# One decoder layer on one core: the per-layer input gets a buffer of its own, and the first norm's rows move from ScalarE's queue to SyncE's

## The chip, the cores and the metric

The kernel runs on 1 core of one Trainium2 chip. Times are device microseconds (us) of one execution, from the device's own clock; the figure that counts is the median of several runs. PE is TensorE (matmuls; PEld its weight loads), ACT is ScalarE, DVE is VectorE, POOL is GpSimd, SP is SyncE, which here only issues transfers (DMAs). SPq, ACTq and POOLq are the queues on which these three engines issue them.

## The reference

One layer of a decoder trunk over 256 positions of width 1024, all in 32-bit floats. Three attention mixers share one projection; their outputs are gated and merged; two norms follow, with a feed-forward block between them that also takes a second, per-layer input `p` (256 positions of width 256):

```python
proj = x @ w_in[i]
...
o_a = dsa_mixer(aq, ak, av, iq, ik, iw, bias_a)
o_b = dilated_mixer(bq, bk, bv, bias_b)
o_c = moba_mixer(cq, ck, cv, bias_c)
gates = jax.nn.sigmoid(x @ w_gate[i]).reshape(bsz, s_len, N_BRANCH, D_MODEL)
merged = (gates[:, :, 0] * (o_a @ w_br_a[i])
          + gates[:, :, 1] * (o_b @ w_br_b[i])
          + gates[:, :, 2] * (o_c @ w_br_c[i]))
x = layer_norm(ALPHA * x + merged @ w_out[i], ln1_g[i], ln1_b[i])
h = jnp.square(jax.nn.relu(x @ w_up[i])) @ w_down[i]
ple = jax.nn.sigmoid(x @ w_ple_gate[i]) * (p[i] @ w_ple[i])
x = layer_norm(ALPHA * x + h + ple, ln2_g[i], ln2_b[i])
```

`w_ple_gate` is called the embedding gate here, and `p @ w_ple` the embedding product.

## The kernel before, in words

**Split operands.** Each 32-bit operand of a matmul is held as two parts: a high part, the value rounded to the narrower matmul format, and a low part, the rest. A product is three matmuls: high by high, high by low, low by high (`prod`, L136). The parts of a weight block are made on the chip. `Weights._split` loads a block of up to 128 x 1024 (512 KB) into `raw` (SP, L71), ACT copies it to the high part `whi` (L75), and DVE, up to the 58th block with POOL for some of the columns, subtracts it to get the low part `wlo` (L79). `raw` and the parts have five buffers each. `Weights.get` keeps some blocks ahead of the matmuls (`AHEAD`, four); a load waits until a `raw` buffer is free, so until its subtraction is done.

**Order.** The order of the work on each engine is made by a scheduler from the program order and priorities; each engine then works through its list strictly in order, and so does each queue of transfers. `issue_after(x)` makes what stands in its block come after the instruction `x` on the engine of `x`.

**The mixers.** Blocks of queries and keys (`feat`) are products of the weights with the input, `q_pair` (ACT L217, DVE L218) and `k_pair` (L228, L229) turn them into pairs, and `logits` (L274) multiplies them. Bias tables T come by DMA from a table in memory (`toeplitz`, three transfers each, L188; three buffers). `attend` transposes the weights of the softmax (L314), copies them into a pair `pt` (ACT L321, DVE L322), multiplies by the values (L324, L325) and adds the parts (ACT L328 and DVE L329 `ov`, DVE L330 `o`); `pair_out` (L333, L334) makes a pair of the result. Between these steps the program puts products of the gates (`fill("g")`, L241), which fill PE's time. After the scores of the indexer comes the second mixer (two rounds of `slots`), then the third mixer (three rounds of `head`), then the first.

**The per-layer input.** Between the second mixer and the third, `p` is loaded into `pr` (SP, L471), and the pair `ph` (ACT, L472) and `pl` (DVE, L473) is made of it. `pr` is a tile of the pool `wk2` under the tag `eb`, so it takes one of the two buffers of that tag, which hold the softmax weights of `slots`; its load waits until the transposes of the second round have read them. `ph` and `pl` are first read more than 100 us later, by the embedding product.

**The end of the first half.** `merge` multiplies the last branch (L582, L583), and makes pairs `q` of the merged values (L586, L587). `outp` is the output projection: eight blocks of `w_out` into four PSUM banks (halves b of the positions, halves c of the columns). `outp.finish` gets the last four blocks, and with them up to four further blocks from the list ahead: both of `w_ple` and the first two of the eight of the embedding gate (`u_pg`). As each bank is complete, `ln1` adds the residual (DVE L646, from PL, which ACT's queue loaded at L614), takes statistics (L623 to L629), a power on POOL (L630), and scales by the norm's two rows (DVE L635, L637); then PE transposes (L656) and a pair `x1` is made (ACT L658, DVE L659). The embedding product (24 matmuls, copied to PL by ACT at L675) fills PE meanwhile; the embedding gate `pg` reads `x1`. After it come 32 blocks of the feed-forward's first product (L705, L707), its second product, and the second norm.

**The rows.** `row_load` (L610) loads the two rows of a norm to all 128 partitions, 1024 KB, on ACT's queue. For the first norm it stands behind the load of the residual, and both are issued after the sixth of the eight high parts of the merge (`muls[5]`).

Of the kernel before, what the change touches and what calls it, by code (L numbers as in the profile page):

```python
# [11 lines left out]
F32 = mybir.dt.float32  # L12
F32R = mybir.dt.float32r
ALU = mybir.AluOpType
# [6 lines left out]
S = 256  # L21
# [10 lines left out]
N_U = 384  # L32
# [17 lines left out]
class Weights:  # L50


    def __init__(self, tc, raw, part):
        self.tc, self.nc = tc, tc.nc
        self.raw, self.part = raw, part
        self.units, self.done, self.parts, self.after = [], 0, {}, ()

    def add(self, src, n, hi=None, lo=None, stage=None, by="v", urgent=0):
        i = len(self.units)
# [3 lines left out]
    def _split(self, i):  # L63
        nc = self.nc
        src, n, hi, lo, r, by, _ = self.units[i]
        if callable(src):
            r = src()
        else:
            if r is None:
                r = self.raw.tile([128, 1024], F32, name="raw", tag="raw")[:, :n]  # L70
            nc.sync.dma_start(r, src)  # L71
        if hi is None:
            hi = self.part.tile([128, 1024], F32R, name="whi", tag="whi")[:, :n]
            lo = self.part.tile([128, 1024], F32R, name="wlo", tag="wlo")[:, :n]
        nc.scalar.copy(hi, r)  # L75
        cut = ((nc.vector, slice(None)),) if by == "v" else (
            (nc.vector, slice(0, by * n // 1024)), (nc.gpsimd, slice(by * n // 1024, n)))
        for e, c in cut:
            low = e.tensor_tensor(lo[:, c], r[:, c], hi[:, c].bitcast(F32), op=ALU.subtract)  # L79
            if e is nc.gpsimd:  # L80
                self.pool = low.ins
        self.parts[i] = (hi, lo)
# [13 lines left out]
def hybrid_layer(ctx: ExitStack, tc: tile.TileContext, x0, xn, pT, wqk, wva, wvb, wg, wbc, wba,  # L96
                 wout, wup, wdq, wdn, wpg, wple, lnrow, rel, mask, out):
    nc = tc.nc
    pe, act, dve, pool = nc.tensor, nc.scalar, nc.vector, nc.gpsimd
# [8 lines left out]
    W = Weights(tc, raw, part)  # L108
# [13 lines left out]
    ph = keep.tile([128, 2, S], F32R, name="ph")  # L122
    pl = keep.tile([128, 2, S], F32R, name="pl")
# [5 lines left out]
    t = banks.tile([128, 512], F32, name="b4", tag="b4")  # L129
# [23 lines left out]
    pm = mid.enter_context(tc.tile_pool(name="pm", bufs=1))  # L153
# [19 lines left out]
    for t in TASKS:  # L173
# [8 lines left out]
        else:  # L182
            u_q.append([add(wqk[int(t) - FIRST], 1024)])

    def toeplitz(h0, step):
        t = tp.tile([128, 3, 256], F32, name="T", tag="T")
        for i in range(3):
            nc.sync.dma_start(t[:, i], bass.AP(  # L188
                tensor=tabd.tensor,
                offset=tabd.offset + (h0 + i * step) * COPIES * N_U + 127,  # L190
                ap=[[N_U - 16, 8], [N_U - 1, 16], [1, 256]]))
        return t


# [87 lines left out]
    op = pm.tile([128, 8, 2, S], F32R, name="op")  # L282
# [20 lines left out]
            dve.tensor_tensor(V[:, b, h0:h0 + heads, DH:128], src,  # L303
                              V[:, b, h0:h0 + heads, 0:DH].bitcast(F32), op=ALU.subtract)

    n_pt = [0]

    def attend(heads, o):

        ts = []  # L310
        for i, (P, vh, h) in enumerate(heads):
            t = next(ps_t)
            for c in (1, 2, 0):
                m = pe.transpose(t[:, 128 * c:128 * c + 128], P[:, 128 * c:128 * c + 128], ident)  # L314
                if i or c != 1:
                    tc.keep_in_program_order(m)
            ts.append(t)
        for t, (P, vh, h) in zip(ts, heads):
            pt = pts[n_pt[0] % 2]
            n_pt[0] += 1  # L320
            act.copy(pt[:, 0], t[:, 0:384])  # L321
            dve.tensor_tensor(pt[:, 1], t[:, 0:384], pt[:, 0].bitcast(F32), op=ALU.subtract)  # L322
            v = next(ps_t).rearrange("p (a s) -> p a s", a=2)
            pe.matmul(v, lhsT=V[:, 0, vh], rhs=pt[:, :, 0:256], start=True, stop=False)  # L324
            pe.matmul(v[:, :, 128:256], lhsT=V[:, 1, vh], rhs=pt[:, :, 256:384], start=False,  # L325
                      stop=True)
            x = wk2.tile([64, 2, S], F32, name="ov", tag="ov")
            act.copy(x, v[64:128])  # L328
            dve.tensor_tensor(x, v[0:64], x, op=ALU.add)  # L329
            dve.tensor_tensor(o[64 * h:64 * h + 64], x[:, 0], x[:, 1], op=ALU.add)  # L330
# [99 lines left out]
    for j in range(4):  # L430
        s = logits(iq[j], kI)
        r = wk2.tile([128, 768], F32, name="ri", tag="eb")
# [23 lines left out]
    for j in range(2):  # L456
# [10 lines left out]
        slots(qs, k, Ts, 1 + 2 * j, o)  # L467
        pair_out(o, 3 + j)
        fill("g")
    pr = wk2.tile([128, 2, S], F32, name="pr", tag="eb")  # L470
    nc.sync.dma_start(pr, pT)  # L471
    act.copy(ph, pr)  # L472
    dve.tensor_tensor(pl, pr, ph.bitcast(F32), op=ALU.subtract)  # L473
    values(u_vb, 384, 5, 6, False)
    fill("g")
    for j in range(3):
# [61 lines left out]
    class Wide:  # L538
# [17 lines left out]
                for c in range(len(self.cut[b])):  # L556
                    self.go(k, b, c)

        def finish(self, ks, done, spare):

            for k in ks:
                self.ws[k] = W.get(self.units[k], min(AHEAD, ks[-1] - k + spare))
            for b in range(2):
                for c in range(len(self.cut[b])):
                    for k in ks:
                        self.go(k, b, c)
                    done(b, c, self.acc[b][c])
# [38 lines left out]
    x1 = p3.tile([128, 2, KT, 2, 128], F32R, name="x1")  # L606
    rows1 = p3.tile([128, 2, D], F32, name="rows", tag="rows")

    def row_load(t, i):
        act.dma_start(t, lnrow[i:i + 2].rearrange("r d -> (r d)").partition_broadcast(128)  # L610
                      .rearrange("p (r d) -> p r d", r=2))

    with tc.issue_after(muls[5]):
        act.dma_start(PL, xn)  # L614
        row_load(rows1, 0)

    st = {}

# [41 lines left out]
        if b == 1:  # L660
            W.after = (i0.ins, i1.ins)

    outp.finish((4, 5, 6, 7), ln1, 5)


    wp = [W.get(u, 0) for u in u_ple]
# [309 lines left out]
```

## Time and profile before

| what | us |
|---|---|
| median of 3 runs (438.4 to 439.96) | 438.52 |
| the profiled execution's own time | 436.83 |
| its span, first to last instruction | 435.0 |
| PE busy | 424.3 |
| DVE busy | 355.3 |
| ACT busy | 274.7 |
| POOL busy | 107.5 |

A profile is one execution, recorded by the hardware. It is read as a page (busy times, the span in 40 slices, the chain of work that ended last, the costliest groups) and by questions to the trace: waits (who waited for whom), timelines of one engine, groups by line, the transfers. Times in a timeline run from the span's start. The profiled execution took 436.83 us; its span of 435.0 leaves out what lies around the instructions. The granted clock of TensorE was 0.996 of full speed over the span. A matmul's recorded time reaches beyond the start of the next, since they are pipelined: from start to start tells more than the length of one.

### The profile page before, as it was taken

To read this page: it belongs to the slowest core of one execution; us is meant where nothing else is said; L and a number is where in the kernel's file an instruction comes from. 1 tells how busy PE (TensorE), PEld (TensorE's weight loads), DVE (VectorE), ACT (ScalarE), POOL (GpSimd) and SP (SyncE) were. 2 spreads that over 40 slices of the span, in tenths; PEclk is the share of its full clock that TensorE was granted. 3 is DMA by queue.
4 is the path that set the end of the run, shared out by engine and by line. 5 is a ranking of instruction groups with operands and counts; after the bars stand their busy time and mean duration, and the time that the engine had idled before them with its cause. 6 is when DMAs were issued, how large, how long until landed. Compare 5 with 4: busy or idle time off the path is not lost.

```text
span 435.0 us, 7673 instructions
## 1 busy us (share of the span) xinstructions
PE 424.3 (98%) x2799; PEld 385.1 (89%) x2799; DVE 355.3 (82%) x625; ACT 274.7 (63%) x490; POOL 107.5 (25%) x98
## 2 busy tenths in 40 slices
PE   8999999999999999999999999999999999999993
PEld 8999999998999999999887888888888888888882
DVE  4978977577666588869988779999988898998984
ACT  6775375585777777746625567778887855665500
POOL 2564355392634656700000000000100000000001
PEclk9999999999999999999999999999999999999998
DMA  8897765465555334474980865656895378758411
GB/s 290 300 330 226 237 182 184 157 201 192 185 166 169 128 112 152 145 199 161 358 335 0 313 219 190 190 182 196 270 281 187 104 202 280 196 195 282 149 42 57
DMA packets 27690, 86.39 MB, mean 199 GB/s; under 512 B 2884, under 2 KB 6892, under 8 KB 27268
## 3 DMA queue, kind: packets, MB, share of 16 engines
q1 hardware_dynamic: 25872, 79.54, 55.5%
q0 software_dynamic: 640, 2.17, 2.8%
q10 hardware_dynamic: 1140, 4.19, 2.7%
q8 instruction: 22, 0.36, 0.3%
q14 instruction: 16, 0.13, 0.1%
HBM read 83.99 MB, written 1.90 MB: 197 GB/s over the span
## 4 chain that ended last, share of the span: by engine, by line
PE 92%; DMA 2%; issue 2%; DVE 2%; ACT 1%; POOLq 0%; POOL 0%; SPq 0%; DVEq 0%
PE mm L136 40%; PE b L136 23%; PE mm L705 14%; PE mm L707 7%; PE b L274 3%; PE b L413 2%; DMA G<-in_x_dram 1%; PE b L314 1%; DMA pr<-in_pT_dram 1%; PE b L324 1%; PE b L325 0%; DVE o L330 0%; DVE ov L329 0%; POOLq L972 0%; POOL rs L630 0%
## 5 line engine op out<-in xcount | busy, mean ns | idle before, releaser
L79 DVE TENSOR_TENSOR wlo<-raw,whi 128x1024 fp32r<-128x1024 f32 (+5 forms) x146 | 158.4, 1096 | 37.3 <-ACT whi L75 32.7
L75 ACT CAST whi<-raw 128x1024 fp32r<-128x1024 f32 (+3 forms) x146 | 146.1, 1011 | 46.6 <-PE b L136 11.7
L79 POOL TENSOR_TENSOR wlo<-raw,whi 128x384 fp32r<-128x384 f32 (+3 forms) x58 | 79.0, 1369 | 81.4 <-ACT whi L75 72.3
L136 PE MATMUL mm<-xl,whi 128*128 128x256 f32 x336 | 95.6, 284 | 0.0
L136 PE MATMUL mm<-xh,whi 128*128 128x256 f32 x336 | 95.0, 283 | 0.0
L136 PE MATMUL mm<-xh,wlo 128*128 128x256 f32 x336 | 94.7, 282 | 0.0
L136 PEld LDWEIGHTS mm<-xl,whi 128*128 128x128 f32 x336 | 63.3, 188 | 1.5
L705 PE MATMUL mm<-x,whi 128*128 128x512 f32 x256 | 64.1, 392 | 0.0
L136 PEld LDWEIGHTS mm<-xh,whi 128*128 128x128 f32 x336 | 63.3, 188 | 0.6
L136 PEld LDWEIGHTS mm<-xh,wlo 128*128 128x128 f32 x336 | 63.3, 188 | 0.3
L705 PEld LDWEIGHTS mm<-x,whi 128*128 128x128 f32 x256 | 46.1, 189 | 8.3
L136 PE MATMUL b<-whi,hT 128*128 128x512 f32 (+2 forms) x164 | 51.8, 381 | 0.0
L707 PEld LDWEIGHTS mm<-x,wlo 128*128 128x128 f32 x256 | 34.9, 190 | 2.5
L753 POOL DMA_DIRECT2D rows<-in_wdq_dram x4 | 3.6, 908 | 135.0 <-DVE wlo L79 81.7
L707 PE MATMUL mm<-x,wlo 128*128 128x256 f32 x256 | 35.7, 282 | 0.0
L136 PEld LDWEIGHTS b<-whi,hT 128*128 128x128 f32 x164 | 30.5, 188 | 5.8
L136 PE MATMUL b<-wlo,hT 128*128 128x512 f32 (+2 forms) x82 | 31.2, 381 | 0.0
L630 POOL TENSOR_TENSOR rs<-rs,half 128x1 f32<-128x1 f32 x4 | 4.1, 1032 | 101.5 <-DVE rs L629 101.5
L710 DVE TENSOR_REDUCE r<-mm 128x256 f32<-128x512 f32 x32 | 22.0, 688 | 5.2 <-PE mm L707 5.2
L241 ACT ACTIVATE G<-mm 128x256 f32<-128x256 f32 x24 | 9.1, 381 | 23.0 <-PE mm L136 22.9
L136 PE MATMUL mm<-op,whi 128*128 128x256 f32 x128 | 23.6, 281 | 0.0
L136 PE MATMUL b<-whi,x 128*128 128x512 f32 x64 | 20.4, 395 | 0.3 <-ACT x L658 0.3
(162 smaller groups left out, 736.6 us busy)
## 6 DMA issues: line engine op xcount, KB each, us to landing
raw<-in_wup_dram SPq DMA_DIRECT2D x32, 512.0 KB
raw<-in_wg_dram SPq DMA_DIRECT2D x24, 512.0 KB
raw<-in_wqk_dram SPq DMA_DIRECT2D x18, 512.0 KB
raw<-in_wdn_dram SPq DMA_DIRECT2D x16, 512.0 KB
raw<-in_wdq_dram SPq DMA_DIRECT2D x12, 512.0 KB
raw<-in_wout_dram SPq DMA_DIRECT2D x8, 512.0 KB
raw<-in_wpg_dram SPq DMA_DIRECT2D x8, 512.0 KB
T<-tabd SPq DMA_DIRECT2D x24, 128.0 KB
```

The costliest lines, as they stand in the source:

```text
L75: nc.scalar.copy(hi, r)
L79: low = e.tensor_tensor(lo[:, c], r[:, c], hi[:, c].bitcast(F32), op=ALU.subtract)
L136: m = pe.matmul(ps, lhsT=a[x], rhs=b[y], start=first and i == 0, stop=last and i == 2)
L241: act.activation(G[:, n_g[0]], ps, AF.Tanh, scale=0.5)
L274: m = pe.matmul(ss[h][:, QC[b]], lhsT=q[d, x, c], rhs=k[d, y, 0:128 * (b + 1)], start=i == 0, stop=i == 2)
L314: m = pe.transpose(t[:, 128 * c:128 * c + 128], P[:, 128 * c:128 * c + 128], ident)
L324: pe.matmul(v, lhsT=V[:, 0, vh], rhs=pt[:, :, 0:256], start=True, stop=False)
L413: pe.matmul(first[f], lhsT=w[:, k, 128 * f:128 * f + 128], rhs=x[:, k], start=k == i == 0, stop=k == KT - 1 and i == 2)
L630: pool.tensor_tensor(rs, rs, half, op=ALU.pow)
L705: pe.matmul(ps, lhsT=hi[:, cs[k]], rhs=x1[:, :, k], start=k == 0, stop=False)
L707: pe.matmul(ps[:, :, 0], lhsT=lo[:, cs[k]], rhs=x1[:, :, k, 0], start=False, stop=k == KT - 1)
L710: dve.tensor_reduce(r, ps.rearrange("p b a t -> p b t a"), axis=AX.X, op=ALU.add)
```

## The change

Two edits. First, `pr` becomes a tile of the pool `pm` with no tag, so with a place of its own. Its load is issued after the last transfer of the last bias table that was asked for (`table[0]`), and `ph` and `pl` are held behind the last copies of a transposed softmax (`cast`). Second, the first norm's rows are no longer loaded by ACT but by SP, and behind the load of the second block of the embedding gate (`W.loads[u_pg[1]]`); `outp.finish` calls this once its blocks have been asked for. The second norm's rows stay on ACT's queue. To have the instructions to refer to, `Weights`, `toeplitz` and `attend` keep what they issue.

```diff
-            nc.sync.dma_start(r, src)
+            self.loads[i] = nc.sync.dma_start(r, src).ins
...
-            nc.sync.dma_start(t[:, i], bass.AP(
+            table[0] = nc.sync.dma_start(t[:, i], bass.AP(
...
-            act.copy(pt[:, 0], t[:, 0:384])
-            dve.tensor_tensor(pt[:, 1], t[:, 0:384], pt[:, 0].bitcast(F32), op=ALU.subtract)
+            cast[0] = act.copy(pt[:, 0], t[:, 0:384]).ins
+            cast[1] = dve.tensor_tensor(pt[:, 1], t[:, 0:384], pt[:, 0].bitcast(F32),
+                                        op=ALU.subtract).ins
...
-    pr = wk2.tile([128, 2, S], F32, name="pr", tag="eb")
-    nc.sync.dma_start(pr, pT)
-    act.copy(ph, pr)
-    dve.tensor_tensor(pl, pr, ph.bitcast(F32), op=ALU.subtract)
+    pr = pm.tile([128, 2, S], F32, name="pr")
+    with tc.issue_after(table[0]):
+        nc.sync.dma_start(pr, pT)
+    with tc.issue_after(cast[0]), tc.issue_after(cast[1]):
+        act.copy(ph, pr)
+        dve.tensor_tensor(pl, pr, ph.bitcast(F32), op=ALU.subtract)
...
-        def finish(self, ks, done, spare):
+        def finish(self, ks, done, spare, loaded):
             for k in ks:
                 self.ws[k] = W.get(self.units[k], min(AHEAD, ks[-1] - k + spare))
+            loaded()
...
-    def row_load(t, i):
-        act.dma_start(t, lnrow[i:i + 2].rearrange("r d -> (r d)").partition_broadcast(128)
+    def row_load(t, i, by=act):
+        by.dma_start(t, lnrow[i:i + 2].rearrange("r d -> (r d)").partition_broadcast(128)
...
         act.dma_start(PL, xn)
-        row_load(rows1, 0)
...
-    outp.finish((4, 5, 6, 7), ln1, 5)
+    def rows_load():
+        with tc.issue_after(W.loads[u_pg[1]]):
+            row_load(rows1, 0, nc.sync)
+
+    outp.finish((4, 5, 6, 7), ln1, 5, rows_load)
```

The scheduler moves instructions at three places. The first is ACT, from the end of the second mixer to the first round of the third (`pt` is the transposed softmax, `ov` and `k` are what the next steps need). Before:

```order
L321 CAST pt_116<-b_1312 128x384
L321 CAST pt_117<-b_1316 128x384
L241 ACTIVATE G<-mm 128x256
L75 CAST whi<-raw 128x1024
L472 CAST ph<-pr 128x512
L328 COPY ov<-b_1322 64x512
L328 COPY ov<-b_1331 64x512
L228 CAST k<-mm 128x256
```

And in the changed program:

```order
L323 CAST pt_116<-b_1312 128x384
L323 CAST pt_117<-b_1316 128x384
L477 CAST ph<-pr 128x512
L243 ACTIVATE G<-mm 128x256
L75 CAST whi<-raw 128x1024
L331 COPY ov<-b_1322 64x512
L331 COPY ov<-b_1331 64x512
L230 CAST k<-mm 128x256
```

The copy to `ph` moves up by two instructions, to stand right behind the copies `pt`. On DVE the subtraction `pl` moves ahead of one `wlo` in the same way.

The second place is SP's queue, from the last blocks of the output projection on. Before:

```order
L71 DMA raw<-in_wout_dram 128x1024 x8
L71 DMA raw<-in_wple_dram 128x1024 x2
L71 DMA raw<-in_wpg_dram 128x1024 x8
L71 DMA raw<-in_wup_dram 128x1024 x28
L752 DMA rows<-in_wdq_dram 128x1024 x2
```

And in the changed program:

```order
L71 DMA raw<-in_wout_dram 128x1024 x8
L71 DMA raw<-in_wple_dram 128x1024 x2
L71 DMA raw<-in_wpg_dram 128x1024 x2
L616 DMA rows<-in_lnrow_dram 128x2048
L71 DMA raw<-in_wpg_dram 128x1024 x6
L71 DMA raw<-in_wup_dram 128x1024 x28
```

The rows stand behind two of the eight blocks of the gate; on ACT the load at L610, which stood between two casts, is gone. Further up on SP, the load of `pr` stands between the first three transfers of a bias table and the next, ahead of the second block of `wvb`, instead of 21 transfers later.

The third place is DVE in the first norm (`b_2936` to `b_2938` are banks of the output projection). Before:

```order
L79 TENSOR_TENSOR hT<-raw,hT 128x1024 x2
L79 TENSOR_TENSOR wlo<-raw,whi 128x1024 x3
L646 SCALAR_TENSOR_TENSOR Y<-PL,b_2936 128x512
L646 SCALAR_TENSOR_TENSOR Y<-PL,b_2937 128x512
L623 BN_STATS st<-Y 128x6
L79 TENSOR_TENSOR wlo<-raw,whi 128x1024
L623 BN_STATS st<-Y 128x6
L646 SCALAR_TENSOR_TENSOR Y<-PL,b_2938 128x512
```

And in the changed program:

```order
L79 TENSOR_TENSOR hT<-raw,hT 128x1024 x2
L79 TENSOR_TENSOR wlo<-raw,whi 128x1024 x4
L651 SCALAR_TENSOR_TENSOR Y<-PL,b_2936 128x512
L651 SCALAR_TENSOR_TENSOR Y<-PL,b_2937 128x512
L628 BN_STATS st<-Y 128x6 x2
L651 SCALAR_TENSOR_TENSOR Y<-PL,b_2938 128x512
```

The fourth `wlo`, that of the second block of the gate, moves from the middle of the statistics to ahead of the first residual sum. On PE the first four transposes of the norm move ahead of the last six matmuls of the embedding product, behind which they stood; ACT's copy of them likewise stands ahead of the last copy to PL.

More of the change, by code (lines that the diff above doesn't have):

```diff
@@ L55, in __init__ @@
         self.raw, self.part = raw, part
-        self.units, self.done, self.parts, self.after = [], 0, {}, ()
+        self.units, self.done, self.parts, self.after, self.loads = [], 0, {}, (), {}
     def add(self, src, n, hi=None, lo=None, stage=None, by="v", urgent=0):
@@ L183, in hybrid_layer @@
             u_q.append([add(wqk[int(t) - FIRST], 1024)])
+    table = [None]
     def toeplitz(h0, step):
@@ L187, in toeplitz @@
         for i in range(3):
-            nc.sync.dma_start(t[:, i], bass.AP(
+            table[0] = nc.sync.dma_start(t[:, i], bass.AP(
                 tensor=tabd.tensor,
                 offset=tabd.offset + (h0 + i * step) * COPIES * N_U + 127,
-                ap=[[N_U - 16, 8], [N_U - 1, 16], [1, 256]]))
+                ap=[[N_U - 16, 8], [N_U - 1, 16], [1, 256]])).ins
         return t
@@ L304, in v_out @@
                               V[:, b, h0:h0 + heads, 0:DH].bitcast(F32), op=ALU.subtract)
-    n_pt = [0]
+    n_pt, cast = [0], [None, None]
     def attend(heads, o):
```

## The prediction

> **What bounds the kernel now.** I read the profile's page first, then the waits of TensorE (PE), then the chain that ended last, then the timelines of single engines around the places that these name. Its first lines say that PE is the bound:
>
> ```profile
> span 435.0 us, 7673 instructions
> PE 424.3 (98%) x2799; PEld 385.1 (89%) x2799; DVE 355.3 (82%) x625; ACT 274.7 (63%) x490; POOL 107.5 (25%) x98
> ```
>
> With 98% of the span busy on PE, a change that takes no matmul away can only win back the time in which PE stood still. The waits of PE list all of it (engine and line, what it waited for: us in total, times, longest):
>
> ```profile
> PE b L131 <- POOL ident masks.py:199: 1.7, 1, 1.7
> PE b L274 <- DVE q L218: 1.1, 1, 1.1
> PE b L136 <- ACT x L658: 0.3, 1, 0.3
> ```
>
> The first lies at the start and isn't touched. The second is the first logits of the third mixer, the third the first matmul of the embedding gate after the norm: one place for each half of the change. The chain that ended last (start, us, what) shows what stood behind the second:
>
> ```profile
> 96.54 5.08 DMA pr<-in_pT_dram
> 101.64 0.63 ACT ph L472
> 102.30 0.69 DVE pl L473
> ...
> 107.13 0.42 DVE q L218
> 107.59 0.96 PE b L274 x12
> 108.55 8.01 PE mm L136 x66
> ```
>
> The load of pr went out at 96.54, when its borrowed buffer came free, and the copy into ph waited for it on ScalarE (ACT), which works in order. Everything queued behind that copy on ACT, and behind pl on VectorE (DVE), came late, the pair q of the logits last.
>
> **Part one: pr's own room.** What it cost is read from PE's timeline (start, us, what; in brackets the idle time and its releaser):
>
> ```profile
> 106.23 0.28 PE L136 MATMUL mm<-xl,whi 128*128 128x256 f32 x1
> 107.59 0.96 PE L274 MATMUL b<-k,q 64*128 64x128 f32 x12 [1.08 <-DVE q L218]
> ```
>
> Matmuls overlap, so the bracket undercounts. From one start to the next are 1.36 us; in the last row of the chain 66 matmuls take 8.01, 0.12 each. Lost are 1.36 - 0.12 = 1.24 us; the least I can read is 1.08. I take 1.24, since it counts the start that failed to come, and keep 1.08 as the low end.
>
> Is all of it won? ACT in the trace:
>
> ```profile
> 95.37 0.86 ACT L321 CAST pt<-b 128x384 fp32r<-128x384 f32 x2
> 96.90 1.05 ACT L75 CAST whi<-raw 128x1024 fp32r<-128x1024 f32 x1
> 101.64 0.62 ACT L472 CAST ph<-pr 128x512 fp32r<-128x512 f32 x1 [3.70 <-DMA pr<-in_pT_dram]
> 102.29 1.07 ACT L328 COPY ov<-b 64x512 f32<-64x512 f32 x2
> 106.47 0.38 ACT L217 ACTIVATE q<-mm 128x256 fp32r<-128x256 f32 x1
> ```
>
> In the new order ph stands right behind the two copies pt, which end at 95.37 + 0.86 = 96.23, so with its data there it ends near 96.9; the gate's activation and the cast of L75 slip by some 0.3 us to 98.2, where nothing waits for them. The copies ov need the second of two matmul pairs:
>
> ```profile
> 99.49 0.28 PE L325 MATMUL b<-pt,V 128*128 128x256 f32 x1
> ```
>
> They can end by about 99.77 + 0.6 = 100.4 instead of 103.36. Behind them come k (0.4) and one cast (1.05): 101.9. Then q, whose sums are complete before 24 gate matmuls and 5 of the next group: 29 x 0.12 = 3.5 us ahead of 106.23, so at 102.7. Its copy and DVE's half (0.38 + 0.42) end near 103.7, an estimate from these rows, 2.5 us before PE asks. What is late next is therefore nothing at this place, with 2.5 us to spare. The cost of the early load: one issue on SyncE (SP) between transfers of the bias tables, and 256 KB of traffic at about 60 us. Behind it stands the second load of the last values' weights:
>
> ```profile
> 58.09 3.23 SPq L188 DMA_DIRECT2D T<-tabd  x5
> 73.69 0.82 ACT L75 CAST whi<-raw 128x768 fp32r<-128x768 f32 x1
> ```
>
> Five tables took 3.23 us to issue, 0.65 each; pr takes the place of one of them ahead of that load, whose cast runs only at 73.69 without a wait. With some 10 us of cover I cost it at nothing; without the cover it would be one such issue, 0.65 us. The DVE half pl (0.69) now stands one place earlier, ahead of a wlo, where DVE was idle anyway. Part one: -1.24.
>
> **Part two: the norm's rows.** The lost time on PE:
>
> ```profile
> 230.89 1.04 PE L656 MATMUL b<-ident,Y 128*128 128x128 f32 x8
> 232.22 0.50 PE L136 MATMUL b<-whi,x 128*128 128x512 f32 x1 [0.29 <-ACT x L658]
> 232.79 0.61 PE L656 MATMUL b<-ident,Y 128*128 128x128 f32 x4
> 233.34 0.73 PE L136 MATMUL b<-whi,x 128*128 128x512 f32 x2
> ```
>
> and the chain's pieces beside it, which price a matmul of the embedding product and a transpose:
>
> ```profile
> 225.61 5.46 PE mm L136 x24
> 235.88 0.44 PE b L656 x4
> ```
>
> Eight transposes should take 0.88 and took 1.33; four should take 0.44 and took 0.55. Lost: 0.45 + 0.11 = 0.56; the bracket alone says 0.29, the low end. The rows load runs on the queue of ACT and lands among the gate's weights (SP and ACT queues, then ACT's casts):
>
> ```profile
> 213.38 0.33 ACTq L610 DMA_DIRECT2D rows<-in_lnrow_dram  x1
> 214.26 0.33 SPq L71 DMA_DIRECT2D raw<-in_wpg_dram  x1
> 216.01 1.06 ACT L75 CAST whi<-raw 128x1024 fp32r<-128x1024 f32 x1 [1.60 <-DMA raw<-in_wple_dram]
> 217.28 1.06 ACT L75 CAST whi<-raw 128x1024 fp32r<-128x1024 f32 x1 [0.21 <-DMA raw<-in_wpg_dram]
> 222.12 1.05 ACT L75 CAST whi<-raw 128x1024 fp32r<-128x1024 f32 x1 [3.78 <-DMA raw<-in_wpg_dram]
> ```
>
> Block 0 came 1.27 us behind the transfer before it, block 1 came 4.84 us behind block 0: in between, the 1024 KB of rows took the engines. The DMA view of 217 to 218 us has no other queue than ACT's (packets, MB, share of 16 engines):
>
> ```profile
> q10 hardware_dynamic: 49, 0.40, 96.2%
> ```
>
> Issued behind block 1 on the same queue, rows can't overtake it. Block 1 then lands near 217.28 + 1.27 = 218.6, and rows, twice the size, near 221.1. DVE:
>
> ```profile
> 217.10 2.50 DVE L79 TENSOR_TENSOR wlo<-raw,whi 128x1024 fp32r<-128x1024 f32 x2 [0.59 <-ACT whi L75]
> 221.11 1.37 DVE L646 SCALAR_TENSOR_TENSOR Y<-PL,b 128x512 f32<-128x512 f32 x2 [1.51 <-PE b L136]
> 223.21 1.23 DVE L79 TENSOR_TENSOR wlo<-raw,whi 128x1024 fp32r<-128x1024 f32 x1
> 226.33 1.41 DVE L635 SCALAR_TENSOR_TENSOR Y<-Y,mv,rows 128x512 f32<-128x512 f32 x2
> 227.65 0.75 DVE L637 SCALAR_TENSOR_TENSOR Y<-Y,rs,rows 128x512 f32<-128x512 f32 x1
> ```
>
> The split of block 1 (1.23) stood inside the norm; now it stands ahead of it. Cast 218.6 to 219.6, split to 220.9, just before the sums of L646 at 221.11: it fits the 1.51 us of idle. The norm's first half is then done at 228.40 - 1.23 = 227.2. PE's order has moved to match: the first four transposes stand ahead of the last 6 of the 24 embedding matmuls, so at 225.4 + 18 x 0.23 = 229.5, and the copy x is made while those 6 run (1.37 us). The next copies come 1.23 us earlier too, more than the 0.56. rows are needed at 226.33 - 1.23 = 225.1, 4 us behind their landing. Part two: -0.56. ACT loses one issue, SP gains one.
>
> One rule speaks against this half. The Trainium skill, in "DMA: Bandwidth & Descriptors", section "Issuing engines are not separate DMA queues", says that transfers of all issuing engines run on the same 16 DMA engines and interleave, and that another issuing engine only saves sequencer time. By it, block 1 would land as before; that is the third rival. The row of q10 differs from it here: for a microsecond only ACT's queue moved data, with a block of SP's outstanding since 214.26.
>
> **The sum.** -1.24 - 0.56 = -1.80, between -1.37 and -1.80 from these rows. Both halves shift everything behind them, because PE waits nowhere else and no wait in these lists is for a fixed time; the end of the program is unchanged. Against the profiled execution that is 436.83 - 1.80 = 435.03; that execution is 1.7 us faster than the median of the runs shown, 438.52, which I use for the forecast: 436.7. That is 0.41% less; 0.5% of 438.52, about what a measurement of this kernel can tell from no change, is 2.2 us.
>
> **The rivals.** First, part one is won and part two isn't: a copy x or its low half is late again, now relative to a PE that comes sooner. For: the chain Y, transposes, x, low half has less than 0.5 us to spare in my reckoning. Against: DVE wins 1.23 there. 438.52 - 1.24 = 437.3. Chance 0.17.
>
> Second, a new wait replaces the one at the logits: with pr gone, the casts of weights ahead of q wait for their own loads, since SP's loads wait for buffers that DVE frees. For: ACT and DVE are in order. Against: these casts had no such wait before, and their loads went out before pr's. Only part two is left: 438.52 - 0.56 = 438.0. Chance 0.08.
>
> Third, on the other side: block 1 lands as late as before, because the queue doesn't decide it, while its split now stands ahead of the norm on DVE. Then the two sums of L646 and the first statistics, which ran before the split (221.11 to 223.1), run after it: the norm is 2.0 us later. The second half's transposes (232.79) are late by that, PE loses about 2.0: 438.52 - 1.24 + 2.0 = 439.3. It decides from a landing of block 1 after about 220.0: 221.11 less cast and split (1.05 + 1.23), plus the 1.23 by which the norm is earlier otherwise. The rule of the Trainium skill quoted above is one that would make this so. Against it stands the row of q10. Chance 0.10.
>
> That the change doesn't do what it says would show as pr still landing at 101.6; its order has the load between the bias tables, so I give that no chance of its own.
>
> **How the numbers follow.** Forecast 0.65, rivals 0.17, 0.08 and 0.10. The three runs of before lie between 438.40 and 439.96, so each case can read up to about 1 us off. The forecast's own range is 436.7 - 0.7 to 437.2 + 0.3; with the rivals and the spread, 435.3 to 439.3. Faster by over 0.5% needs 0.4 us more than the sum: 0.26, nearly all out of the forecast. Slower by over 0.5% (over 440.7) needs the third rival and a high reading: 0.06. Within: 0.68.
>
> **What would show it.** Right: no idle of ACT before ph, ph near 96 us, no PE wait at the logits of the third mixer, block 1's cast before 220, its split ahead of L646 (L651 in the changed file), PE's wait before the gate under 0.1 us. Wrong: a PE wait of more than 0.5 us at either place or at a new one, a cast that waits for block 1 beyond 220, or a gain that the profile shows at 235 us and no longer at the end.

## The result, and the profile after

The changed kernel takes 435.68 us (median of 11 runs, 435.02 to 436.84), the kernel before, run beside it, 438.36 us (437.36 to 442.55). The ratio is 0.9932, 95% interval 0.9908 to 0.9957: 2.68 us less in the medians, where 1.80 were forecast, and 0.68% by the ratio, where it was 0.41%. The profiled execution of the changed kernel took 436.27 us with a span of 434.5 us; that of before took 436.83 us, less than any of the 11 runs of before timed beside the changed kernel. So the two profiles, side by side, differ by 0.56 us, far less than the medians, and much of what follows turns on that.

The page of the changed kernel, and the waits of PE in it (what it waited for: us in total, times, longest):

```profile
span 434.5 us, 7670 instructions
PE 424.8 (98%) x2799; PEld 385.8 (89%) x2799; DVE 353.9 (81%) x625; ACT 274.9 (63%) x490; POOL 107.3 (25%) x98
```

```profile
PE b L131 <- POOL ident masks.py:199: 1.7, 1, 1.7
PE b L661 <- DVE Y L642: 0.3, 1, 0.3
```

The wait at the third mixer's logits is gone. The one at the gate isn't: it has moved from the copy x to the transposes (L661, L656 before), and is as long as it was.

At the first place ACT's timeline (start, us, what; in brackets the idle time before it) shows no wait ahead of `ph`:

```profile
96.03 0.86 ACT L323 CAST pt<-b 128x384 fp32r<-128x384 f32 x2
96.77 0.65 ACT L477 CAST ph<-pr 128x512 fp32r<-128x512 f32 x1
99.88 1.18 ACT L331 COPY ov<-b 64x512 f32<-64x512 f32 x2 [1.24 <-PE b L328]
104.22 0.38 ACT L219 ACTIVATE q<-mm 128x256 fp32r<-128x256 f32 x1
```

The copy stands right behind `pt` and runs at once, and `ov` now waits for PE, not PE for it. PE's timeline at the logits:

```profile
106.78 0.27 PE L136 MATMUL mm<-xh,wlo 128*128 128x256 f32 x1
106.98 0.95 PE L276 MATMUL b<-k,q 64*128 64x128 f32 x12
```

From one start to the next are 0.20 us, where it had been 1.36.

At the second place, SP's queue and ACT's casts:

```profile
211.28 2.81 SPq L71 DMA_DIRECT2D raw<-in_wpg_dram  x2
214.14 0.42 SPq L616 DMA_DIRECT2D rows<-in_lnrow_dram  x1
```

```profile
215.84 1.06 ACT L75 CAST whi<-raw 128x1024 fp32r<-128x1024 f32 x1 [0.23 <-DMA raw<-in_wpg_dram]
219.80 1.05 ACT L75 CAST whi<-raw 128x1024 fp32r<-128x1024 f32 x1 [2.91 <-DMA raw<-in_wpg_dram]
```

Block 1 is issued ahead of the rows, and its cast still starts 3.96 us behind that of block 0 (4.84 before). DVE has to take that block ahead of the norm:

```profile
220.89 1.23 DVE L79 TENSOR_TENSOR wlo<-raw,whi 128x1024 fp32r<-128x1024 f32 x1 [2.62 <-ACT whi L75]
222.03 1.28 DVE L651 SCALAR_TENSOR_TENSOR Y<-PL,b 128x512 f32<-128x512 f32 x2
227.11 0.75 DVE L642 SCALAR_TENSOR_TENSOR Y<-Y,rs,rows 128x512 f32<-128x512 f32 x1
```

The sums of L651 start at 222.03. In before they started at 221.11, as soon as PE had them ready, and PE is 0.50 us earlier here by the start of the embedding product (224.94 against 225.44): they could have started near 220.6. DVE stood idle for 2.62 us in front of the split instead. So the first half of the norm won only about 0.5 us (227.11 against 227.65), as much as PE came earlier.

All the profiles of this study can be laid side by side, because PE's program falls into stretches that hardly vary by themselves. The marks are starts in PE's timeline: the first product of a weight block (the first L136 of 256 columns, near 17 us), the third mixer's first logits, the first matmul of the embedding product, the first matmul of the feed-forward (L705 before), and the end of the last matmul. The stretch from the feed-forward on takes 172.16 or 172.17 us in all 14 profiles, so it is left out; A runs from the first mark to the logits (place of part one), B from there to the embedding product, C from there to the feed-forward (place of part two). The last column is how far the cast of the gate's block 1 starts behind that of block 0.

| profile | first mark | A | B | C | block 1 behind block 0 |
|---|---|---|---|---|---|
| before | 16.68 | 90.91 | 117.85 | 29.81 | 4.84 |
| after | 17.34 | 89.64 | 117.96 | 29.78 | 3.96 |
| e1, part one alone | 17.63 | 89.65 | 117.89 | 30.15 | 5.89 |
| e2, part two alone | 16.71 | 91.00 | 117.83 | 29.10 | 1.90 |
| e3, late copy | 17.69 | 89.64 | 117.96 | 34.00 | 8.04 |
| e4, before again | 17.30 | 91.81 | 119.34 | 30.98 | 6.04 |
| e5, after again | 17.23 | 89.63 | 117.96 | 30.00 | 3.90 |
| e6, part one alone | 17.51 | 89.64 | 117.96 | 32.75 | 6.52 |
| e7, rows ahead | 17.61 | 89.65 | 117.89 | 30.07 | 5.26 |
| e8, split on POOL | 16.83 | 89.63 | 117.90 | 29.10 | 2.68 |
| e9, part two alone | 17.31 | 91.30 | 117.79 | 29.10 | 1.97 |
| e10, after, third | 16.82 | 89.64 | 117.89 | 30.17 | 4.07 |
| e11, split on POOL | 16.65 | 89.65 | 117.89 | 29.10 | 4.30 |
| e12, late block | 17.00 | 89.65 | 117.89 | 29.83 | 5.63 |

The first mark wanders by 1.04 us (16.65 to 17.69) whatever the kernel; before's profile had one of the earliest, after's a later one by 0.66. Apart from that, A has a floor of 89.63 to 89.65 and C one of 29.10.

### The profile page after: what moved, and what is told of

Same layout as the page of the kernel before. It is cut to its first block, busy times and chain, and to the rows that moved or that the text cites. A ratio compares the mean times of both kernels' runs of the same rounds, so it can differ in the third digit from the quotient of the medians.

```text
span 434.5 us, 7670 instructions
## 1 busy us (share of the span) xinstructions
PE 424.8 (98%) x2799; PEld 385.8 (89%) x2799; DVE 353.9 (81%) x625; ACT 274.9 (63%) x490; POOL 107.3 (25%) x98
## 3 DMA queue, kind: packets, MB, share of 16 engines
q0 software_dynamic: 640, 2.17, 2.8%
## 4 chain that ended last, share of the span: by engine, by line
PE 87%; DVE 4%; DMA 4%; issue 2%; ACT 0%; POOLq 0%; POOL 0%; SPq 0%; DVEq 0%
PE mm L136 40%; PE b L136 18%; PE mm L714 14%; PE mm L716 7%; PE b L276 3%; PE b L416 2%; DMA raw<-in_wpg_dram 2%; DMA G<-in_x_dram 1%; PE b L316 1%; DMA raw<-in_wout_dram 1%; PE b L327 1%; DVE st L628 1%; DVE Y L642 1%; DVE Y L651 1%; PE b L328 0%
## 5 line engine op out<-in xcount | busy, mean ns | idle before, releaser
L136 PE MATMUL mm<-xl,whi 128*128 128x256 f32 x336 | 95.7, 285 | 0.0
L136 PE MATMUL mm<-xh,whi 128*128 128x256 f32 x336 | 94.9, 283 | 0.0
L136 PE MATMUL mm<-xh,wlo 128*128 128x256 f32 x336 | 94.7, 282 | 0.0
L136 PEld LDWEIGHTS mm<-xl,whi 128*128 128x128 f32 x336 | 63.3, 188 | 1.6
L136 PEld LDWEIGHTS mm<-xh,whi 128*128 128x128 f32 x336 | 63.3, 188 | 0.4
L136 PEld LDWEIGHTS mm<-xh,wlo 128*128 128x128 f32 x336 | 63.3, 188 | 0.3
L136 PE MATMUL b<-whi,hT 128*128 128x512 f32 (+2 forms) x164 | 51.8, 381 | 0.0
L136 PEld LDWEIGHTS b<-whi,hT 128*128 128x128 f32 x164 | 30.5, 188 | 5.8
L136 PE MATMUL b<-wlo,hT 128*128 128x512 f32 (+2 forms) x82 | 31.2, 381 | 0.0
L136 PE MATMUL mm<-op,whi 128*128 128x256 f32 x128 | 23.6, 281 | 0.0
L136 PE MATMUL b<-whi,x 128*128 128x512 f32 x64 | 20.3, 394 | 0.0
```

Of the source, the lines that this page charges most:

```text
L136: m = pe.matmul(ps, lhsT=a[x], rhs=b[y], start=first and i == 0, stop=last and i == 2)
```

## The experiments

Each kernel was timed in five rounds beside the kernel before. Theory: both parts work by taking a wait for a transfer out of an in-order engine's list, part one on ACT and part two on DVE. The main rivals were that the room and the early transfer matter in part one, and that the queue doesn't decide when block 1 lands in part two.

**e1_pr_only.** The changed program with the rows back on ACT's queue:

```diff
         act.dma_start(PL, xn)
+        row_load(rows1, 0)
...
-    outp.finish((4, 5, 6, 7), ln1, 5, rows_load)
+    outp.finish((4, 5, 6, 7), ln1, 5, lambda: None)
```

> The first half of the change alone: pr in a room of its own, loaded early; the rows stay on ScalarE's queue. Theory A (the two profiles tell the whole: the wait at the logits was worth 1.2 us and the second half nothing): 1.2 us less than before, ratio 0.9973, no PE wait at the logits, the wait at the first norm as before (0.3 us). Rival B (the second half carries the rest of the measured 2.7 us): also 1.2 us less. Rival C (the load of pr costs more in most executions than in the profiled one of before): 2.4 us or more less, ratio 0.9945 or below.

Measured: 436.92 us against 438.08, ratio 0.997 (0.9953 to 0.9986). A fell to its floor, 89.65. That is part one's 1.2 us.

**e2_rows_only.** The changed program with `pr` back in the borrowed buffer and its copy back in place.

```diff
-    pr = pm.tile([128, 2, S], F32, name="pr")
-    with tc.issue_after(table[0]):
-        nc.sync.dma_start(pr, pT)
-    with tc.issue_after(cast[0]), tc.issue_after(cast[1]):
-        act.copy(ph, pr)
-        dve.tensor_tensor(pl, pr, ph.bitcast(F32), op=ALU.subtract)
+    pr = wk2.tile([128, 2, S], F32, name="pr", tag="eb")
+    nc.sync.dma_start(pr, pT)
+    act.copy(ph, pr)
+    dve.tensor_tensor(pl, pr, ph.bitcast(F32), op=ALU.subtract)
```

> The second half alone: the first norm's rows issued by SyncE behind the second block of the embedding gate; pr as before. Theory A: no change within 0.4 us, since the split of the second block now holds up the norm by about what its removal from the norm's chain wins. Rival B: 1.4 us less, ratio 0.9968. Rival C: no change. In all three the PE wait at the third mixer's logits stays at about 1.1 us in the profile.

Measured: 437.23 us against 438.08, ratio 0.9985 (0.9967 to 1.0003). The interval reaches 1, and the 0.85 us of the medians lie between what the theory (0.4 at most) and the rival (1.4) expected, so this run alone doesn't decide; e9 repeats it. C is 29.10, 0.71 under before's. In this profile the forecast's picture came true: block 1's cast at 218.33, its split before the norm, and no wait at the gate.

**e3_copy_late.** The kernel before, with `pr` in the borrowed buffer and its late load; only the copy and the subtraction move, behind the first pair q of the third mixer:

```diff
-    act.copy(ph, pr)
-    dve.tensor_tensor(pl, pr, ph.bitcast(F32), op=ALU.subtract)
...
         q = q_pair(feat(14 + 2 * j))
+        if j == 0:
+            with tc.issue_after(last[0]), tc.issue_after(low[0]):
+                act.copy(ph, pr)
+                dve.tensor_tensor(pl, pr, ph.bitcast(F32), op=ALU.subtract)
```

> The kernel before with pr still in its borrowed buffer and loaded as late as before; only the copy to ph and the subtraction pl are moved behind the first q of the third mixer. If the cost was ScalarE waiting in order on a load that nobody else needed yet, this wins what the first half of the change wins: 1.2 us less (2.4 by rival C) and no PE wait at the logits. If the place of the load among the other transfers or the borrowed buffer was the cost, no change: within 0.4 us.

Measured: 436.9 us, ratio 0.9975 (0.9951 to 1.0). Its profile has the load at its old place, and still the floor of A:

```profile
97.56 0.38 SPq L471 DMA_DIRECT2D pr<-in_pT_dram  x1
```

```profile
104.46 0.38 ACT L217 ACTIVATE q<-mm 128x256 fp32r<-128x256 f32 x1
104.74 0.61 ACT L480 CAST ph<-pr 128x512 fp32r<-128x512 f32 x1
```

So neither the room nor the early transfer is what part one wins by: it is that ACT no longer stands in front of a copy whose data isn't there, with work behind it that PE needs. Either cure is worth the same 1.2 us.

**e4_before_again.** The kernel before with a constant written differently (`NEG = -1.0e30`), to see how far two profiles of one program differ.

> The kernel before once more (one constant written differently, same value): ratio 1.000 within 0.2%, about 438.4 us in the median. Theory A: its profiled execution is nearer to 438 than to 436.8 us, and the excess over the profile of before lies where no part of the change reaches, for instance before the first products, up to 1.5 us. Rival B: the excess lies at the first norm, between 221 and 236 us. Rival C: it lies at the load of pr, between 96 and 108 us.

Measured: 438.46 us, ratio 1.0016 (0.9993 to 1.0039). Its profile, of an execution of 440.97 us, has both waits again, and longer:

```profile
PE b L274 <- DVE q L218: 2.0, 1, 2.0
PE b L656 <- DVE Y L637: 0.9, 1, 0.9
```

The logits waited 2.0 us here, not 1.1. And the wait had a second price. PE's time by stretches (us, PE busy, granted clock, DMA share, GB/s):

```profile
106.00:108.00 2.00, 1.13 (x10) 1.00 0.03 8
108.00:110.00 2.00, 0.89 (x12) 0.94 0.19 49
110.00:112.00 2.00, 2.00 (x12) 0.50 0.56 213
112.00:114.00 2.00, 2.00 (x15) 0.71 0.80 262
114.00:116.00 2.00, 2.00 (x20) 1.00 0.78 244
```

After 4 us in which PE was busy for 2.02, the granted clock fell to 0.50, and it was back from 114 on. At those clocks 6 us lose 0.06 x 2 + 0.50 x 2 + 0.29 x 2 = 1.7 us, beside the wait itself; B, otherwise within 0.17 us, was some 1.5 longer. The expectation that the excess over the first profile lies where the change doesn't reach was wrong: of the 4.2 us of span, 0.62 lie ahead of the first mark, 0.90 + 1.49 in the wait at the logits and the slow clock behind it, and 1.17 at the norm.

**e5_after_again and e10_after_third.** The changed kernel with the same constant written differently, in two later batches.

> The changed kernel once more, with nothing but a constant written in another way (minus 1.0e30). It gives a second profile and a second time of the whole change, beside the kernel that has part one alone. My theory: 435.7 us, ratio to the kernel before 0.993 to 0.996, no wait of PE at the third mixer's logits; the stretch from the first embedding product to the first up product 29.1 to 29.8 us, with the cast of the gate's second block starting between 218 and 220.5. The rival that the whole is worth more than its parts: a ratio of 0.992 or less again while part one alone stays at 0.997.

> The whole change a third time, as the reference for the two kernels beside it: 435.7 us, ratio 0.993. The cast of the gate's second block starts at 219 to 220.5 and its split holds the norm's first instruction up to about 222, as in both profiles so far.

Measured: 435.66 against 438.40, ratio 0.9928 (0.9901 to 0.9956), and 435.73 against 438.06, ratio 0.9935 (0.9913 to 0.9957). In both profiles, as in the first, block 1 comes 3.9 to 4.1 us behind block 0 and its split holds the norm up; C is 30.00 and 30.17, where 29.1 to 29.8 were expected of e5. The changed kernel doesn't reach the floor of C.

**e6_pr_only_again.** The kernel of e1, beside e5.

> Part one alone again (own room and early load of the per-layer input; the norm's rows stay on ScalarE's queue), on the chip of the run above. Theory: 436.9 us, ratio 0.997, so 0.5 to 0.9 us behind the whole change; the cast of the gate's second block starts after 222. Rival: part two is worth nothing in the whole, then it stands within 0.3 us of the run above; or part two is worth 1.2 us and more, then it is that far behind.

Measured: 436.99 against 438.40, ratio 0.9957 (0.9936 to 0.9979); it stands 1.33 us behind the whole change, more than the 0.5 to 0.9 expected. Its profile is that of the slowest of its twelve runs (439.38 us), so it shows not the usual loss but what this stretch can cost. Block 1 comes late, its split waits in the middle of the norm, and PE stands and then slows down:

```profile
223.18 1.05 ACT L75 CAST whi<-raw 128x1024 fp32r<-128x1024 f32 x1 [5.46 <-DMA raw<-in_wpg_dram]
```

```profile
222.06 0.69 DVE L629 BATCH_NORM_STATS2 st<-Y 128x6 f32<-128x512 f32 x1
224.26 1.23 DVE L79 TENSOR_TENSOR wlo<-raw,whi 128x1024 fp32r<-128x1024 f32 x1 [1.51 <-ACT whi L75]
225.40 0.69 DVE L629 BATCH_NORM_STATS2 st<-Y 128x6 f32<-128x512 f32 x1
```

```profile
230.00:232.00 2.00, 1.71 (x13) 1.00 0.00 0
232.00:234.00 2.00, 0.84 (x4) 1.00 0.00 0
234.00:236.00 2.00, 2.00 (x9) 0.69 0.00 0
236.00:238.00 2.00, 2.00 (x6) 0.50 0.00 0
238.00:240.00 2.00, 2.00 (x12) 0.95 0.00 0
```

The second statistics had nothing to do with block 1, but DVE's list put the split between them. C is 32.75: 3.65 over the floor, of which PE's waits of 1.2 us (for Y) and 0.3 us (for x) and the low clock (0.31 x 2 + 0.50 x 2 + 0.05 x 2 = 1.7) make 3.2.

**e7_rows_ahead.** The changed kernel with the rows one place earlier on SP, behind block 0 and ahead of block 1:

```diff
-        with tc.issue_after(W.loads[u_pg[1]]):
+        with tc.issue_after(W.loads[u_pg[0]]):
```

> The whole change, but the rows of the norm (1 MB) are issued by SyncE ahead of the gate's second block, not behind it. Theory (a queue serves its transfers in the order of their issue, so the block waits for the rows in front of it): the cast of the second block starts at 221.5 us or later, as in the kernel before (222.1), 4.5 us and more behind that of the first block; the time falls back by 0.3 to 0.8 us against the whole change, to 436.0 to 436.6. Rival (the 16 engines share their time among all that is outstanding, the place in the queue doesn't matter): the cast starts at 219 to 220.5 as with the whole change, and the time stays within 0.2 us of it.

Measured: 436.21 us, ratio 0.9941 (0.9921 to 0.9961), 0.55 behind e5 in the medians. Queue and cast:

```profile
211.52 0.33 SPq L71 DMA_DIRECT2D raw<-in_wpg_dram  x1
211.90 0.42 SPq L616 DMA_DIRECT2D rows<-in_lnrow_dram  x1
214.00 1.46 SPq L71 DMA_DIRECT2D raw<-in_wpg_dram  x2
```

```profile
222.10 1.05 ACT L75 CAST whi<-raw 128x1024 fp32r<-128x1024 f32 x1 [4.21 <-DMA raw<-in_wpg_dram]
```

One place in one queue moves the cast from 219.80 to 222.10. Of these 2.3 us, 1.0 is already there at block 0 (216.84 against 215.84), and 1.3 lie between the two blocks (5.26 against 3.96). The rows were also issued 2.1 us ahead of block 1 here (211.90 against 214.00). So the place in the queue matters. (The scheduler also put the split back into the middle of the norm here, so the time is not that of the place alone; the landing is.)

**e8_split_pool and e11_split_pool_again.** The changed kernel, with the subtraction for block 1 on POOL, so that DVE's list holds nothing of block 1 ahead of the norm:

```diff
+        if by == 0:
+            cut = ((nc.gpsimd, slice(None)),)
...
-    u_pg = [add(wpg[i], 1024) for i in range(8)]
+    u_pg = [W.add(wpg[i], 1024, by=0 if i == 1 else "v") for i in range(8)]
```

> The whole change, with the low half of the gate's second block made by GpSimd, not VectorE, so that VectorE goes from the last output products straight to the first norm whatever the block does. Theory (what is left of the second part's loss is the wait of VectorE for the block ahead of the norm): the norm's first instruction no longer waits for the block, the stretch from the first embedding product to the first up product is 29.1 us or shorter, and the time is 0.2 to 0.7 us below the whole change, 435.0 to 435.5. GpSimd's instruction takes about 3.0 us by its rows of 240 and 384 columns (1116 and 1456 ns) and ends before 224.6, when the power of the first half is asked for. Rival: it ends later, or slows VectorE while both run; then the power of the first half (L637) waits for it, PE waits for the norm by 0.5 us or more, and the time is the same or higher.

> The whole change with the low half of the gate's second block on GpSimd, again. In its first profile the block also landed earlier (218.1 against 219.9), so the split and the landing weren't told apart. Theory (VectorE's wait for the block ahead of the norm costs time): 435.2 us, 0.3 to 0.6 us below the whole change beside it, even where the block lands at 219 to 220.5 again. Rival (the first measurement was the early landing): within 0.2 us of the whole change.

Measured: 435.20 us (ratio 0.9919, 0.9892 to 0.9946) and 435.15 us (0.9919, 0.9886 to 0.9951), each time below the changed kernel beside it, by 0.46 and 0.58 us in the medians. In the first profile block 1 also came early; in the second it came as late as in the changed kernel, and C is 29.10 all the same. ACT, DVE and POOL of the second:

```profile
219.65 1.05 ACT L75 CAST whi<-raw 128x1024 fp32r<-128x1024 f32 x1 [3.24 <-DMA raw<-in_wpg_dram]
```

```profile
219.86 1.37 DVE L653 SCALAR_TENSOR_TENSOR Y<-PL,b 128x512 f32<-128x512 f32 x2 [2.19 <-PE b L138]
```

```profile
220.84 2.40 POOL L81 TENSOR_TENSOR wlo<-raw,whi 128x1024 fp32r<-128x1024 f32 x1 [36.43 <-ACT whi L75]
223.87 1.01 POOL L637 TENSOR_TENSOR rs<-rs,half 128x1 f32<-128x1 f32 x1 [0.63 <-DVE rs L636]
```

The norm's first sums wait for PE alone and start 2.2 us earlier than in the profile of the changed kernel (1.4 us, once PE's own lead of 0.75 at the embedding product, 224.19 against 224.94, is taken off), while the cast is as late as there. POOL is done 0.63 us before the power is asked of it. This is the fastest version of the study: its 13 runs lie between 434.66 and 435.88 us. The two intervals overlap those of the changed kernel, so its lead rests on two batches, the profiles and the spread.

**e9_rows_only_again.** The kernel of e2.

> Part two alone again, since its first measurement (0.9985, from 0.9967 to 1.0003) is smaller than the 1.3 us by which the whole change stood below part one alone on one chip (435.66 against 436.99). Theory: the first measurement was low by chance within its interval; 437.0 us, ratio 0.996 to 0.9975. Rival: part two is worth about 0.6 us alone and more only when part one is there; then 437.4 us and more, ratio 0.998 to 0.999.

Measured: 436.59 us against 438.06, ratio 0.9959 (0.9925 to 0.9993). Part two alone is worth 0.85 us in one batch and 1.47 in the other, a little more than expected; the two intervals overlap, so the runs don't tell whether it is worth as much alone as on top of part one. C is at its floor in both profiles.

**e12_late_block_free.** Part one; the rows stay on ACT's queue, so block 1 lands late; its load is issued where it was, but its cast and split are traced behind the first half's norm:

```diff
         act.dma_start(PL, xn)
+        row_load(rows1, 0)
...
+        if b == 0:
+            with tc.issue_after(normed[1]):
+                W.split(u_pg[1])
...
     def rows_load():
-        with tc.issue_after(W.loads[u_pg[1]]):
-            row_load(rows1, 0, nc.sync)
+        W.load(u_pg[1])
...
-    outp.finish((4, 5, 6, 7), ln1, 5, rows_load)
+    outp.finish((4, 5, 6, 7), ln1, 3, rows_load)
```

(`W.load` issues the transfer into a `raw` buffer, `W.split` makes the two parts of it later.)

> Part one, with the norm's rows left on ScalarE's queue, so that the gate's second block lands late, and with its split placed on VectorE behind the first half's norm, so that the norm doesn't wait for it. Theory (what part two is worth is that VectorE's in-order queue waits inside the norm for a block that is not needed yet): the cast starts at 222 to 224.5, no instruction of the first half's norm waits for it, and the time is 435.3 to 435.9 us, as with the whole change, 1.1 us and more below part one alone. Rival (the late block itself costs, or the 1 MB on ScalarE's queue): 436.6 to 437.0, as part one alone, with PE waiting at the gate's second product.

Measured: 435.8 us, ratio 0.9937 (0.9912 to 0.9961), the time of the changed kernel beside it (435.73).

```profile
221.56 1.05 ACT L75 CAST whi<-raw 128x1024 fp32r<-128x1024 f32 x1 [4.57 <-DMA raw<-in_wpg_dram]
```

```profile
220.21 1.37 DVE L663 SCALAR_TENSOR_TENSOR Y<-PL,b 128x512 f32<-128x512 f32 x2 [1.96 <-PE b L147]
225.38 0.75 DVE L654 SCALAR_TENSOR_TENSOR Y<-Y,rs,rows 128x512 f32<-128x512 f32 x1
227.30 1.22 DVE L79 TENSOR_TENSOR wlo<-raw,whi 128x1024 fp32r<-128x1024 f32 x1
```

Block 1 is later than in any profile of the changed kernel, the 1 MB is back on ACT's queue, and the time is no longer than the changed kernel's: the norm's first half runs past the block. (It is not free: C is 29.83, 0.73 over its floor, with a PE wait of 0.2 us for x.) So part two isn't worth what the landing is worth. It is worth that DVE, in order, doesn't wait inside the norm.

## Why the prediction was right, and where not

**Part one: right in mechanism and size.** The forecast was 1.24 us. In the profiles A falls from 90.91 to 89.64, by 1.27, and in the medians part one is worth 1.16 (e1) and 1.41 (e6). Two estimates on the way were good to 0.2 us once the first mark's 0.66 us is taken off: `ph` ends at 97.4 (forecast 96.9), `ov` at 101.1 (100.4). The pair q is done at 104.88 + 0.41 = 105.3 (103.7), so 0.9 us later than worked out, and 1.7 us before PE asks, not 2.5. The working left out a copy that stands ahead of q on ACT, that of the mixer's output pair, which waits for DVE:

```profile
103.91 0.41 ACT L336 CAST op<-o 128x256 fp32r<-128x256 f32 x1 [1.50 <-DVE o L333]
```

The early load cost nothing that shows.

**Part two: the step that failed is the landing.** The forecast had block 1 land near 218.6, 1.3 us behind block 0, its split done by 220.9, and the norm start at 221.1. In the profile the cast starts at 219.80, the split ends at 222.1 and the norm starts at 222.03. In three profiles of the changed kernel block 1 comes 3.9 to 4.1 us behind block 0. By the forecast's own bound, 220.0 (219.5 here, where PE is 0.50 earlier), that is about where nothing is lost and nothing won: C stays at 29.78 to 30.17, where the forecast's 0.56 off 29.81 is 29.25. The premise that a block behind another in one queue follows it at the distance of the one before it was wrong. With part two alone it held much better (1.90, 1.97), though SP issues the block at the same distance ahead of PE's embedding product (11.2 us in e2 and in after).

The trace tells what came late. A block travels in 128 packets of 4 KB, the rows in 128 of 8 KB, and a transfer reports its end in sixteen parts; the cast waits for the last of them. In the profile of the changed kernel fifteen parts of block 1 had landed by 218.01, inside the forecast, and the sixteenth at 219.71; in e2 the fifteenth landed at 217.97 and the sixteenth at 218.23. The packets from 217 to 218 and from 218 to 219 us, in the changed kernel and then in e2 (those under 512 B are reports):

```profile
DMA packets 48, 0.35 MB, mean 348 GB/s; under 512 B 2, under 2 KB 2, under 8 KB 9
DMA packets 48, 0.37 MB, mean 373 GB/s; under 512 B 0, under 2 KB 0, under 8 KB 5
```

```profile
DMA packets 81, 0.44 MB, mean 442 GB/s; under 512 B 16, under 2 KB 16, under 8 KB 38
DMA packets 51, 0.42 MB, mean 418 GB/s; under 512 B 0, under 2 KB 0, under 8 KB 0
```

In the changed kernel 39 and then 43 packets of the rows moved while the last part of block 1 was still out. So the premise that the rows can't overtake a block issued ahead of them on the same queue was wrong: the queue is in order by issue, not by landing. In all four profiles where block 1 comes 3.90 to 4.30 us behind (after, e5, e10, e11), one 4 KB packet between the two landings took 1.15 to 1.66 us, where the median packet takes 0.16; in the three with 1.90 to 2.68 (e2, e9, e8) none there took over 0.45. What holds that packet up stays open. Part one need not have to do with it: e8 and e11 are the same kernel, with part one in it, and one has the slow packet and the other not.

Two of the signs that the prediction named fit this. Block 1's cast before 220 came true by 0.2 us, and PE's wait before the gate, to be under 0.1 us, is 0.3.

**The third rival's rule.** The trace had to decide between a queue that orders its transfers and engines that share among all. Seven profiles with the rows on SP behind block 1 have it 1.90 to 4.30 us behind block 0; the one with the rows on SP ahead of it, 5.26; six with the rows on ACT's queue, 4.84 to 8.04. In five of these six the rows were also issued ahead of block 1, by 0.06 to 0.88 us; in e4 they were issued 0.13 us behind it (217.40 against 217.27), and it still came 6.04 us behind block 0, so an earlier issue isn't the whole of it, as far as one profile can tell. So transfers of another issuing engine do delay the block. The Trainium skill says in "DMA: Bandwidth & Descriptors", section "Issuing engines are not separate DMA queues", that they run on the same 16 engines and interleave; the trace agrees. What I drew from that rule, that moving the rows couldn't help, doesn't follow: behind the block in the block's own queue they delay it less.

**Where the extra 0.9 us came from.** The forecast took both waits from one execution, the fastest shown of before. The other profiles show it was a mild one. A is over its floor by 1.27, 1.36, 1.66 and 2.17 us in the four profiles with the old copy, not always by 1.24. C is over its floor by 0.71, 1.05, 1.88, 3.65 and 4.90 in the five with the rows on ACT and the split inside the norm (before, e1, e4, e6, e3), median 1.88; in the three of the whole change by 0.68, 0.90 and 1.07. The difference of those medians, 1.88 - 0.90 = 1.0 us, is about what part two is worth in the times (0.85 and 1.47 alone; 1.33 between e6 and e5). The times are the better measure: the profiles of e3, e4 and e6 are of runs 2.4 to 4.0 us above the medians of their kernels. Even in the profile that the forecast used, the loss by the floor of C was 0.71, not 0.56. The term that was mis-sized is part two, 0.56 for about 1.2: not because the norm became as fast as forecast, but because a wait that varied, up to 4.9 us with the low clock behind it, became one that is short each time. The runs agree: before ranges over 5.2 us in its 11 runs, the changed kernel over 1.8 (1.5 and 2.8 in its other two batches). So that the total came near owes something to luck: part two gained, but not in the way that was worked out. 1.3 + 1.2 = 2.5 lies among the 2.33 to 2.74 measured in three batches.

The first rival's weak place (less than 0.5 us to spare in the norm's chain) was real: in the changed kernel PE waits there by 0.3 to 0.7 us. The second rival didn't appear; no cast ahead of q waits for a load.

## What to carry to other kernels

An instruction that waits for a transfer, on an engine that works in order, costs what stands behind it: look in the trace not for late data but for what is queued behind the wait, and either bring the data earlier or move the instruction back to where it is needed (e3 and e12 move no transfer, and win as much as the part that they stand in for). Then ask whether a wait's length depends on a landing: one profile shows one draw, so price it from several, or from the spread of the times. And if an idle engine can do the step off the critical list, as POOL does in e11, the landing stops mattering.

## What the runs showed of the hardware

**A short wait of PE can cost twice.** In e4 a PE wait of 2.0 us was followed by 6 us at a granted clock of 0.50 to 0.94, in e6 one of 1.2 us, with one of 0.3 shortly before, by 6 us at 0.50 to 0.95, and in e3 one of 1.8 us, with one of 0.6 before it, by 4 us at 0.59 and 0.56; each cost another 1.7 us. Waits of 1.1 (before), 1.2 (e2) and 1.5 us (e9) were not followed by any. PE was busy for 2.02 of 4 us ahead of the drop in e4 and for 1.71 + 0.84 = 2.55 in e6; in e9, which had no drop, for 1.13 + 1.39 = 2.52:

```profile
106.00:108.00 2.00, 1.13 (x10) 1.00 0.03 8
108.00:110.00 2.00, 1.39 (x16) 1.00 0.53 90
```

So neither the length of the wait nor the busy share of 4 us, cut like this, tells the cases apart, and where the bound lies isn't settled. The Trainium skill, "TensorE: Matmul & The Clock Gate", section "What's actually happening", describes half rate after an idle window of about 3.4 us that runs freely. The half rate agrees with the 0.50 here; a wait of that length stands before none of the three drops, the longest was 2.0 us.

**POOL beside DVE.** A subtraction of 128 x 1024 took POOL 2.40 us (1.23 on DVE), less than the 3.0 worked out from its narrower ones, by a profile that is rough on POOL. In e11 the two statistics that DVE ran wholly beside it took 1.28 us together and the sum behind them 0.67, as in the changed kernel without it: these operations show no slowing.
